# Fewer certain experts, tests ahead of the last one, and an accumulation moved from GpSimd to VectorE

## The chip, the cores and the metric

The kernel runs on one core of a Trainium2 chip. The metric is the device time of one execution in microseconds (us), the median of several runs. The engines are TensorE (PE in the profile, with PEld for its weight loads), VectorE (DVE), ScalarE (ACT), GpSimd (POOL) and SyncE (SP). SP issues nearly all large transfers from device memory.

## What is computed

The reference is a network of two layers on 256 tokens of 1024 numbers in float32. In both layers a mixer is followed by a layer of 16 experts.

```python
for i in range(DEPTH):                                   # 2 layers
    sh1, sc1, g1, sh2, sc2, g2 = split(silu(c) @ mod_w[i] + mod_b[i])     # the modulation, 6 vectors
    h = x * (1 + sc1) + sh1
    y = attention_group_mixer(h, ...) if i == 0 else hyena_mixer(h, ...)
    x = layer_norm(ALPHA * x + g1 * y)
    f = moe_ffn(x * (1 + sc2) + sh2, router_w, router_bias, w_gate[i], w_up[i], w_down[i])
    x = layer_norm(ALPHA * x + g2 * f)
# moe_ffn: each token goes to the 2 best experts of its best group of 4; for an expert e
#   out += weight * ((silu(xb @ w_gate[e]) * (xb @ w_up[e])) @ w_down[e])
# hyena_mixer: h @ w_in, a short convolution, two long convolutions through the spectra of a small filter network, @ w_out
```

One expert has three matrices of 4 MB. How many tokens each expert gets follows from the inputs. The reference's routing, worked out on its own inputs, gives experts 0 and 1 of layer 0 28 and 1 tokens, and the other fourteen, sorted, 171, 128, 42, 41, 30, 29, 16, 13, 6, 3, 2, 1, 1, 0. In layer 1 it is 2 and 1, and 215, 184, 33, 30, 18, 14, 6, 5, 3, 1, 0, 0, 0, 0.

## The kernel before

**Stages.** The first 230 us are attention with the modulation woven in. `mod_vec` fetches each of ten modulation vectors in four 1 MB tiles; step `i` scales the two halves of a tile (`k`) by a column of `cz` and adds them up. Four of the eight products per vector are multiplied and added on VectorE (L268, the pairs in `MOD_DVE`), four are scaled on ScalarE (L270), and two of those are then added on GpSimd (L272). GpSimd also adds the two partial sums (L274). The attention units (`diff_scores`, `win_scores`) stand between these steps in the same queues. Then come `mixer_tail` (projection, norm, routing), the experts of layer 0 (`moe`), the hyena mixer, its `mixer_tail`, the experts of layer 1 and the last norm.

**Experts.** `moe` takes positions `p`. Positions 0 and 1 are experts 0 and 1. The two most loaded others are done densely in pieces, beside p = 1 to 8 (`PIECES`: `dense_up` on odd p, four more tiles; `dense_down` on even p, two more tiles). Positions 2 to 13 are the other twelve, by falling load, so p = 9, 10, 11, 12, 13 stand for 3, 2, 1, 1, 0 tokens in layer 0 and 1, 0, 0, 0, 0 in layer 1. An expert takes twelve tiles of 1 MB, eight for gate and up, four for down. Positions 0 to 11 (`RARE = 12`) always run. They are pipelined: `E.up()`, the `back()` of the one before, the `pick()` and `turn_in()` of the next one, dense piece, `E.weights_in()`, `E.down()`. Positions 12 and 13 stand in `rare`, each inside a test on its number of tokens (`tc.If`, L793), the second nested in the first. Every engine takes the test in its own queue.

**Tiles.** Weight tiles go through a ring of 12 slots, with `MORE` extra slots during `moe` (3 in layer 0, 5 in layer 1). SP issues loads in program order through `load` (L143) and waits at each until its slot is free, so it runs ahead by as many tiles as there are slots.

**Fillers.** In layer 0, `filler(p)` computes the spectra of the hyena filter. `filt_mlp` runs at p = 0, and eight pieces `filt_spec` (L1186, L1195, the copies L163 and a store to `spec`) run at the positions in `FILL`. They take PSUM banks from the rotating counter `abank()`, six per piece. `spec_loads` brings each piece's inputs through GpSimd's queue, one piece ahead.

**After the experts.** The first tile of the hyena weights (`hy_w_in`) is asked for at the end of `moe` (`NAHEAD = 1`), the others in `win_loads`. At the start of the hyena stage the residual `xs` is multiplied and shifted by a norm's gain (L1339, L1340).

Of the kernel before, what the change touches and what calls it, by code (L numbers as in the profile page):

```python
# [12 lines left out]
ALU = mybir.AluOpType  # L13
AX = mybir.AxisListType
ET = mybir.EngineType
# [13 lines left out]
MORE = [3, 5]  # L29
# [11 lines left out]
FILL = [0, 8, 9, 9, 10, 10, 11, 11]  # L41
# [5 lines left out]
MOD_DVE = {(1, 0), (2, 0), (2, 1), (3, 0)}  # L47

RARE = 12
NAHEAD = 1  # L50
# [26 lines left out]
def emit(tc, I, O):  # L77
# [4 lines left out]
    with es:  # L82
# [170 lines left out]
        def mod_vec(l, v):  # L253
# [7 lines left out]
            def step(i):  # L261
                w = st[i]
                c_ = [cz[:, 2 * i + k, 0:1] for k in range(2)]
                if i == 0:
                    st["acc"] = w
                for k in range(2):
                    if (i, k) in MOD_DVE:
                        dve.scalar_tensor_tensor(out=st["acc"][:, 0], in0=w[:, k], scalar=c_[k], in1=st["acc"][:, 0], op0=ALU.mult, op1=ALU.add)  # L268
                    else:
                        act.activation(w[:, k], w[:, k], AF.Copy, scale=c_[k])  # L270
                        if i:
                            pool.tensor_tensor(out=st["acc"][:, 1], in0=st["acc"][:, 1], in1=w[:, k], op=ALU.add)  # L272
                if i == 3:
                    pool.tensor_tensor(out=st["acc"][:, 1], in0=st["acc"][:, 1], in1=st["acc"][:, 0], op=ALU.add)  # L274
# [449 lines left out]
        def moe(l, h2, R, first, filler):  # L724
            with tc.tile_pool(name=f"mp{l}", bufs=2, reuse_waits="tile") as mp:
# [26 lines left out]
                hid, last = {}, None  # L752
                for p in range(RARE):
                    if p == 0:
                        E.w = first
                    else:
                        ix = number(1, place(p), [ET.SP], NE - 1) if p > 1 else 1
                        E.w = expert_loads(l, ix, have=second if p == 1 else (), most=8)
                        if p in PIECES:
                            r, half, down = PIECES[p]  # L760
                            dw = dense_loads(l, number(1, 2 + r, [ET.SP], NE - 1), half, down)
                        E.w = expert_loads(l, ix, have=E.w)
                    E.up()
                    if last:
                        last.back()
                    nxt = expert(p + 1) if p + 1 < RARE else None
                    if nxt:
                        nxt.pick()
                    if p == 0:
                        for t in range(2):  # L770
                            dve.tensor_tensor(out=xs[:, t, :], in0=h2[:, t, :], in1=lng, op=ALU.mult)
                            for hf in range(2):
                                s_ = slice(512 * hf, 512 * hf + 512)
                                dve.tensor_tensor(out=xs[:, t, s_], in0=xs[:, t, s_], in1=lnb[hf], op=ALU.add)
                    E.turn_mid()
                    if p in PIECES:
                        if down:
                            dense_down(mp, E.bank, dw, hid[r], R["wtP"][:, :, 2 + r:3 + r], g2b)
                        else:
                            hid[r] = dense_up(mp, E.bank, dw, h2T)  # L780
                    if filler:
                        filler(p)
                    if nxt:
                        nxt.turn_in()
                    E.weights_in()
                    E.down()
                    E, last = nxt, E
                last.back()

# [21 lines left out]
                def beyond():  # L811
# [3 lines left out]
                    with tc.For_i(0, NE):  # L815
# [12 lines left out]
                        dve.tensor_copy(ints[:, :, 0:15], ni[:, :, 1:16])  # L828
                        for i, nm in enumerate(("rankP", "wtP")):
                            dve.tensor_copy(mv_[:, 2 * i:2 * i + 2], R[nm])  # L830
                            dve.tensor_copy(R[nm][:, :, 0:15], mv_[:, 2 * i:2 * i + 2, 1:16])
                        dve.tensor_copy(mv_[:, 4], cap)
                        dve.tensor_copy(cap[:, 0:15], mv_[:, 4, 1:16])
                rare(RARE)
# [343 lines left out]
        def filt_spec(o, q):  # L1178
# [4 lines left out]
            for t in range(2):  # L1183
                b = abank()
# [16 lines left out]
        def filler(p):  # L1201
# [3 lines left out]
            for i in [i for i, p_ in enumerate(FILL) if p_ == p]:  # L1205
                filt_spec(*oq[i])
# [6 lines left out]
        with tc.tile_pool(name="fp", bufs=1, reuse_waits="tile", side="right") as fp:  # L1213
            wi = I["hy_w_in"][0]
            moe(0, h2, R, first, filler)
            ws0 = [win_tile(0, i, -1) for i in range(NAHEAD)]
# [3 lines left out]
        if True:  # L1220
            hTh = hm([128, KC, N], "hTh")
            with tc.tile_pool(name="s1a", bufs=1) as sa:
# [65 lines left out]

                def fwd(src, sp_, s):
# [20 lines left out]
                    for c, op in enumerate((ALU.add, ALU.subtract)):  # L1310
                        dve.tensor_tensor(out=Y[:, c], in0=prods[0], in1=prods[1], op=op)
# [26 lines left out]
                for t in range(2):  # L1338
                    dve.tensor_tensor(out=xs[:, t, :], in0=xs[:, t, :], in1=gb[:, 0], op=ALU.mult)  # L1339
                    dve.tensor_tensor(out=xs[:, t, :], in0=xs[:, t, :], in1=gb[:, 1], op=ALU.add)  # L1340
# [104 lines left out]
```

## Time and profile before

| | us |
|---|---|
| median of 3 runs (1373.05 to 1373.99) | 1373.26 |
| the profiled execution | 1371.12 |
| its span, first to last instruction | 1369.4 |
| PE busy in the span | 1201.0 |
| VectorE busy | 568.1 |
| ScalarE busy | 233.1 |
| GpSimd busy | 122.8 |

All durations below come from the one profiled execution, which is 2.1 us below the median. A busy PE is not a PE at its peak, and a high share over the whole span says little here, since the stages have different limits. So the profile is read by stage.

### The profile page before, as it was taken

The page shows a single profiled execution, that of the slowest core. Times are in us where ns is not written, and L with a number is a line of the kernel's source. Part 1 is how long each engine was busy: PE and PEld are TensorE (multiplying, and loading weights), DVE is VectorE, ACT ScalarE, POOL GpSimd, SP SyncE. Part 2 cuts the span into 40 slices and gives each one's busy share as a digit, 9 for nine tenths or more (in the row PEclk, how much of TensorE's full clock was granted, in tenths as well). Part 3 has the DMA queues.
Part 4 walks back from the last instruction along what each step waited for, and adds up shares of the span by engine and source line. Part 5 has one row for each costly group of instructions (what it writes and reads, how often), then busy time and mean ns, then how long its engine had stood idle before and what let it go on. Part 6 is the DMA issues. An engine that isn't in the chain of part 4 may idle for free. (4 is left out here: it accounts for less than half of the span.)

```text
span 1369.4 us, 21175 instructions
## 1 busy us (share of the span) xinstructions
PE 1201.0 (88%) x8630; PEld 716.2 (52%) x8630; DVE 568.1 (41%) x1127; ACT 233.1 (17%) x441; POOL 122.8 (9%) x118
## 2 busy tenths in 40 slices
PE   5999887958999999899786699996999999999864
PEld 1444444425746566484554387853744747465421
DVE  2466988373031222303333479937122131321313
ACT  2344556130000000000000263203000000000000
POOL 1244433110000000000111000001000000000000
PEclk9999999978999999999999799997999999999985
DMA  9999775576998999999999764687999899999994
GB/s 327 398 369 340 289 285 198 203 275 267 383 402 334 362 401 408 401 391 402 399 400 407 281 229 177 264 311 274 404 409 402 335 403 378 402 403 407 409 408 174
DMA packets 139803, 469.37 MB, mean 343 GB/s; under 512 B 8655, under 2 KB 10279, under 8 KB 139696
## 3 DMA queue, kind: packets, MB, share of 16 engines
q1 hardware_dynamic: 133696, 451.93, 85.0%
q0 software_dynamic: 4928, 13.44, 2.9%
q10 hardware_dynamic: 1072, 2.54, 0.5%
q8 instruction: 71, 1.16, 0.3%
q14 instruction: 36, 0.29, 0.1%
HBM read 462.62 MB, written 5.26 MB: 342 GB/s over the span
## 5 line engine op out<-in xcount | busy, mean ns | idle before, releaser
L642 PE MATMUL acc<-w,xe 128*32 128x256 f32 (+1 forms) x2944 | 228.5, 414 | 12.6 <-DMA w<-in_exp_w_up 5.1
L705 PE MATMUL acc<-xnT,w 128*128 128x256 f32 x1024 | 222.5, 379 | 1.1 <-DVE xs L686 1.1
L705 PEld LDWEIGHTS acc<-xnT,w 128*128 128x128 f32 x1024 | 193.9, 190 | 27.5 <-DVE xs L686 1.3
L642 PEld LDWEIGHTS acc<-w,xe 128*32 128x32 f32 (+1 forms) x2944 | 104.5, 116 | 121.9 <-issue 54.7
L661 PE MATMUL acc<-w,aT 128*32 128x256 f32 (+1 forms) x1472 | 122.8, 421 | 18.2 <-DVE stg L163 8.4
L717 PE MATMUL acc<-w,hid 128*128 128x512 f32 x256 | 111.4, 593 | 0.3 <-DVE xs L686 0.3
L661 PEld LDWEIGHTS acc<-w,aT 128*32 128x32 f32 (+1 forms) x1472 | 52.8, 116 | 75.8 <-issue 26.1
L708 DVE TENSOR_TENSOR hid<-hid,acc 128x256 f32<-128x256 f32 x32 | 13.4, 420 | 189.6 <-ACT hid L707 189.6
L686 DVE TENSOR_TENSOR xs<-xs,acc 128x512 f32<-128x512 f32 x100 | 62.6, 682 | 53.7 <-PE acc L680 53.4
L717 PEld LDWEIGHTS acc<-w,hid 128*128 128x128 f32 x256 | 48.0, 190 | 58.3 <-issue 56.9
L268 DVE SCALAR_TENSOR_TENSOR w<-w,cz 128x1024 f32<-128x1024 f32 x40 | 69.4, 1734 | 13.1 <-DMA w<-in_mod_w 11.4
L646 DVE TENSOR_TENSOR ac<-ac,acc 128x256 f32<-128x256 f32 (+1 forms) x25 | 11.6, 464 | 151.4 <-PE acc L642 151.4
L918 PE MATMUL acc<-w,hT 128*128 128x512 f32 (+1 forms) x192 | 72.6, 524 | 1.7 <-DVE mr L163 1.7
L1268 PE MATMUL acc<-hTh,w 128*128 128x256 f32 x320 | 59.4, 285 | 0.1
L272 POOL TENSOR_TENSOR w<-w 128x1024 f32<-128x1024 f32 x20 | 49.5, 2477 | 104.4 <-ACT w L270 71.3
L645 ACT ACTIVATE ac<-acc 128x256 f32<-128x256 f32 (+1 forms) x25 | 10.4, 418 | 282.4 <-PE acc L642 282.4
L161 ACT ACTIVATE xg<-mis 128x256 f32<-128x256 f32 (+1 forms) x25 | 10.4, 417 | 270.3 <-PE mis L610 270.2
L719 DVE SCALAR_TENSOR_TENSOR do<-acc,wtP,g2b 128x512 f32<-128x512 f32 x32 | 24.0, 751 | 67.7 <-PE acc L717 67.7
L918 PEld LDWEIGHTS acc<-w,hT 128*128 128x128 f32 x192 | 34.9, 190 | 32.2 <-issue 27.7
L610 PE MATMUL mis<-h,Pu 128*32 128x256 f32 (+1 forms) x368 | 38.5, 434 | 14.7 <-DVE PT L163 9.7
L1268 PEld LDWEIGHTS acc<-hTh,w 128*128 128x128 f32 x320 | 49.4, 188 | 2.3 <-ACT ed L1296 1.3
L680 PE MATMUL acc<-yb,PT 32*128 32x256 f32 (+1 forms) x368 | 45.6, 443 | 4.4 <-DVE yb L666 4.4
(351 smaller groups left out, 1398.0 us busy)
## 6 DMA issues: line engine op xcount, KB each, us to landing
w<-in_exp_w_up SPq DMA_DIRECT2D x116, 1024.0 KB, 18.1
w<-in_exp_w_gate SPq DMA_DIRECT2D x116, 1024.0 KB, 18.1
w<-in_exp_w_down SPq DMA_DIRECT2D x116, 1024.0 KB, 13.8
w<-in_mod_w SPq DMA_DIRECT2D x40, 1024.0 KB, 8.2
w<-in_hy_w_in SPq DMA_DIRECT2D x12, 1024.0 KB, 9.7
w<-in_attn_w_in SPq DMA_DIRECT2D x9, 1024.0 KB, 10.5
w<-in_mod_w SPq DMA_DIRECT2D x16, 512.0 KB, 10.8
w<-in_attn_w_out SPq DMA_DIRECT2D x4, 1024.0 KB, 5.0
```

The lines of the kernel that those rows point to most:

```text
L268: dve.scalar_tensor_tensor(out=st["acc"][:, 0], in0=w[:, k], scalar=c_[k], in1=st["acc"][:, 0], op0=ALU.mult, op1=ALU.add)
L272: pool.tensor_tensor(out=st["acc"][:, 1], in0=st["acc"][:, 1], in1=w[:, k], op=ALU.add)
L610: pe.matmul(gb[S * j:S * j + S, 0:nn], Pu[:, t, 0:S], self.h2[:, t, nn * j:nn * j + nn], start=(t == 0), stop=(t == 1), tile_position=(0, ...
L642: pe.matmul(A[m][S * j:S * j + S, 0:nn], self.xe[:, kc, :], w[:, nn * j:nn * j + nn], tile_position=(0, S * j), start=(kc == 0), stop=(kc ...
L661: pe.matmul(y[S * q:S * q + S, 0:nn], lhs, w[:, nn * q:nn * q + nn], tile_position=(0, S * q), start=(kc == 0), stop=(kc == KC - 1))
L680: pe.matmul(o, self.PT[r, 128 * t:128 * t + 128], self.yb[r, 0:nn], start=True, stop=True, tile_position=(S * q, 0))
L686: dve.tensor_tensor(out=x_, in0=x_, in1=o, op=ALU.add)
L705: pe.matmul(b[:, N * m:N * m + N], ws[m][kc // 4][:, kc % 4, 128 * fb:128 * fb + 128], h2T[:, kc, :], start=(kc == 0), stop=(kc == KC - 1))
L717: pe.matmul(b, hid[:, fb, 128 * t:128 * t + 128], ws[fb // 2][:, fb % 2, s_], start=(fb == 0), stop=(fb == 3))
L719: dve.scalar_tensor_tensor(out=o, in0=b, scalar=wt[:, t], in1=g2b[:, s_], op0=ALU.mult, op1=ALU.mult)
L918: pe.matmul(bank[:, 0:width], hT[:, kc, 128 * t:128 * t + 128], st["w"][kc // per][:, kc % per, :], start=(kc == 0), stop=(kc == KC - 1))
L1268: pe.matmul(b[:, 0:N], w_, m, start=(kc == 0 and i == 0), stop=(kc == KC - 1 and i == len(ps) - 1))
```

## The change

`RARE` becomes 10, so positions 10 to 13 are nested tests, and they stand ahead of position 9 (`NEST`), the last certain one. The `back()` of position 8 comes ahead of them, and position 9 is picked after them. `NAHEAD` becomes 4: four hyena tiles are asked for behind position 9's. `MORE` for layer 0 is 4. `FILL` spreads the pieces over p = 0, 0, 4, 6, 8, 8, 9, 9, and these take banks 3, 4 and 5 of the expert. In `mod_vec` ScalarE scales only the two halves of the first tile, and VectorE does all else. The `xs` operations of the hyena stage are placed behind the last operation of the first `fwd`. `beyond` now rotates its tables fully, since it is no longer the last in its layer.

```diff
-MORE = [3, 5]
+MORE = [4, 5]
-FILL = [0, 8, 9, 9, 10, 10, 11, 11]
+FILL = [0, 0, 4, 6, 8, 8, 9, 9]
-MOD_DVE = {(1, 0), (2, 0), (2, 1), (3, 0)}
-RARE = 12
-NAHEAD = 1
+RARE = 10
+NEST = 9
+NAHEAD = 4
...
-                    if (i, k) in MOD_DVE:
-                        dve.scalar_tensor_tensor(out=st["acc"][:, 0], in0=w[:, k], scalar=c_[k], in1=st["acc"][:, 0], op0=ALU.mult, op1=ALU.add)
+                    if i:
+                        dve.scalar_tensor_tensor(out=st["acc"][:, k], in0=w[:, k], scalar=c_[k], in1=st["acc"][:, k], op0=ALU.mult, op1=ALU.add)
                     else:
                         act.activation(w[:, k], w[:, k], AF.Copy, scale=c_[k])
-                        if i:
-                            pool.tensor_tensor(out=st["acc"][:, 1], in0=st["acc"][:, 1], in1=w[:, k], op=ALU.add)
                 if i == 3:
-                    pool.tensor_tensor(out=st["acc"][:, 1], in0=st["acc"][:, 1], in1=st["acc"][:, 0], op=ALU.add)
+                    dve.tensor_tensor(out=st["acc"][:, 1], in0=st["acc"][:, 1], in1=st["acc"][:, 0], op=ALU.add)
...
                 for p in range(RARE):
+                    if p == NEST:
+                        last.back()
+                        last = None
+                        rare(RARE)
+                        E = expert(p)
+                        E.pick()
+                        E.turn_in()
...
-                    nxt = expert(p + 1) if p + 1 < RARE else None
+                    nxt = expert(p + 1) if p + 1 < RARE and p + 1 != NEST else None
...
-                        filler(p)
+                        filler(p, E.bank)
...
-                rare(RARE)
...
-                b = abank()
+                b = bank[4 + t]
...
-                b = abank()
+                b = bank[3 + c % 3]
...
-                    ws = [win_tile(s, i) if s or i >= NAHEAD else ws0[i] for i in range(2)]
+                    ws = [ws0[j] if j < NAHEAD else win_tile(s, j % 2) for j in (2 * s, 2 * s + 1)]
...
-                for t in range(2):
-                    dve.tensor_tensor(out=xs[:, t, :], in0=xs[:, t, :], in1=gb[:, 0], op=ALU.mult)
-                    dve.tensor_tensor(out=xs[:, t, :], in0=xs[:, t, :], in1=gb[:, 1], op=ALU.add)
+                with tc.issue_after(st_["last"]):
+                    for t in range(2):
+                        dve.tensor_tensor(out=xs[:, t, :], in0=xs[:, t, :], in1=gb[:, 0], op=ALU.mult)
+                        dve.tensor_tensor(out=xs[:, t, :], in0=xs[:, t, :], in1=gb[:, 1], op=ALU.add)
```

## Rows read from the trace of the kernel before

**Rows 1.** Busy time by stretch: start:end, length, busy us (count) per engine, granted clock, DMA.

```profile
117.00:232.00 115.00, 94.00 (x445) 52.45 (x443) 106.28 (x179) 68.59 (x135) 48.31 (x24) 1.00 0.73 266
...
411.00:445.00 34.00, 34.00 (x158) 22.72 (x155) 4.01 (x7) 1.96 (x4) 0.00 (x0) 1.00 0.84 334
...
650.00:768.00 118.00, 91.43 (x980) 56.76 (x976) 37.83 (x80) 5.12 (x11) 15.80 (x26) 0.96 1.01 394
...
813.00:892.00 79.00, 74.34 (x489) 60.99 (x488) 78.38 (x112) 28.44 (x47) 0.00 (x0) 0.99 0.59 218
...
1257.00:1351.00 94.00, 70.63 (x776) 31.45 (x776) 19.69 (x37) 5.12 (x11) 0.00 (x0) 0.89 0.98 391
```

**Rows 2.** DMA issues of the page: out<-in, engine, count, KB each, us to landing.

```profile
w<-in_exp_w_up SPq DMA_DIRECT2D x116, 1024.0 KB, 18.1
```

**Rows 3.** Instructions in time, VectorE, 136 to 146 us: start, us, what, idle before.

```profile
136.48 2.30 DVE L987 TENSOR_SCALAR mx<-mx 128x2 f32<-128x2 f32 x1
...
140.57 0.14 DVE L987 TENSOR_SCALAR mx<-mx 128x2 f32<-128x2 f32 x1
...
141.95 1.27 DVE L268 SCALAR_TENSOR_TENSOR w<-w,cz 128x1024 f32<-128x1024 f32 x1
...
145.09 3.44 DVE L268 SCALAR_TENSOR_TENSOR w<-w,cz 128x1024 f32<-128x1024 f32 x1
```

**Rows 4.** The same view for GpSimd, same stretch.

```profile
145.08 2.37 POOL L272 TENSOR_TENSOR w<-w 128x1024 f32<-128x1024 f32 x1 [6.32 <-issue]
```

**Rows 5.** VectorE's groups, 117 to 240 us: count, busy us, mean ns, idle before.

```profile
L268 DVE SCALAR_TENSOR_TENSOR w<-w,cz 128x1024 f32<-128x1024 f32 x24 | 38.5, 1603 | 0.1
...
L393 DVE TENSOR_SCALAR fold<-modc 128x8 f32<-128x8 f32 x2 | 1.8, 914 | 0.0
```

**Rows 6.** GpSimd's busy time of L272 alone, then of L274 alone, 117 to 232 us.

```profile
117.00:232.00 115.00, 29.91 (x12) 1.00 0.73 266
...
117.00:232.00 115.00, 14.14 (x6) 1.00 0.73 266
```

**Rows 7.** PE in time at p = 11 of layer 0: fillers, then down.

```profile
724.38 1.89 PE L1186 MATMUL acc<-fwo,hs 128*128 128x256 f32 x8
...
740.76 3.66 PE L661 MATMUL acc<-w,aT 128*32 128x256 f32 x64 [2.68 <-DVE stg L163]
```

**Rows 8.** SP's issues in time around position 12 of layer 0.

```profile
715.57 1.20 SPq L143 DMA_DIRECT2D w<-in_exp_w_gate  x1
...
737.37 14.56 SPq L143 DMA_DIRECT2D w<-in_exp_w_down  x4
773.84 2.48 SPq L143 DMA_DIRECT2D w<-in_hy_w_in  x4
```

**Rows 9.** The tests, 700 to 780 us: durations min/median/max ns, first and last start; SP's waits.

```profile
L793 SPq COMPARE_BRANCH  x3: 38/48/50, 714.6 to 768.8; - x3
...
SPq L143 <- PEq L793: 4.7, 1, 4.7
```

**Rows 10.** PE and VectorE in time, end of layer 0's experts.

```profile
768.27 1.07 PE L661 MATMUL acc<-w,aT 128*32 128x256 f32 x16 [1.55 <-SPq L793]
769.89 1.15 PE L680 MATMUL acc<-yb,PT 32*128 32x256 f32 x16 [0.55 <-DVE yb L666]
...
771.05 2.48 DVE L686 TENSOR_TENSOR xs<-xs,acc 128x512 f32<-128x512 f32 x4 [1.22 <-PE acc L680]
...
778.92 0.41 DVE L386 TENSOR_SCALAR hT<-mis,fold 128x128 f32<-128x128 f32 x1 [0.36 <-DMA w<-in_hy_w_in]
```

**Rows 11.** PE in time, layer 1: end of p = 8, then p = 10, then p = 11.

```profile
1279.22 0.71 PE L680 MATMUL acc<-yb,PT 32*128 32x256 f32 x6 [0.55 <-DVE yb L666]
...
1305.95 1.07 PE L642 MATMUL acc<-w,xe 128*32 128x256 f32 x16 [1.01 <-DMA w<-in_exp_w_gate]
...
1350.57 1.93 PE L661 MATMUL acc<-w,aT 128*32 128x256 f32 x16 [0.58 <-SPq L793]
```

**Rows 12.** VectorE in time, start of the hyena stage.

```profile
781.77 1.23 DVE L1339 TENSOR_TENSOR xs<-xs,gb 128x1024 f32<-128x1024 f32 x1 [1.28 <-DMA gb<-in_ln_g]
```

More of the change, by code (lines that the diff above doesn't have):

```diff
@@ L831, in beyond @@
                             dve.tensor_copy(R[nm][:, :, 0:15], mv_[:, 2 * i:2 * i + 2, 1:16])
+                            dve.tensor_copy(R[nm][:, :, 15:16], mv_[:, 2 * i:2 * i + 2, 0:1])
                         dve.tensor_copy(mv_[:, 4], cap)
                         dve.tensor_copy(cap[:, 0:15], mv_[:, 4, 1:16])
-                rare(RARE)
+                hid, last = {}, None
+                for p in range(RARE):
+                    if p == NEST:
[5 more added lines that the diff above has]
+                        E.turn_in()
+                    if p == 0:
+                        E.w = first
+                    else:
+                        ix = number(1, place(p), [ET.SP], NE - 1) if p > 1 else 1
+                        E.w = expert_loads(l, ix, have=second if p == 1 else (), most=8)
+                        if p in PIECES:
+                            r, half, down = PIECES[p]
+                            dw = dense_loads(l, number(1, 2 + r, [ET.SP], NE - 1), half, down)
+                        E.w = expert_loads(l, ix, have=E.w)
+                    E.up()
+                    if last:
+                        last.back()
+                    nxt = expert(p + 1) if p + 1 < RARE and p + 1 != NEST else None
+                    if nxt:
+                        nxt.pick()
+                    if p == 0:
+                        for t in range(2):
+                            dve.tensor_tensor(out=xs[:, t, :], in0=h2[:, t, :], in1=lng, op=ALU.mult)
+                            for hf in range(2):
+                                s_ = slice(512 * hf, 512 * hf + 512)
+                                dve.tensor_tensor(out=xs[:, t, s_], in0=xs[:, t, s_], in1=lnb[hf], op=ALU.add)
+                    E.turn_mid()
+                    if p in PIECES:
+                        if down:
+                            dense_down(mp, E.bank, dw, hid[r], R["wtP"][:, :, 2 + r:3 + r], g2b)
+                        else:
+                            hid[r] = dense_up(mp, E.bank, dw, h2T)
+                    if filler:
+                        filler(p, E.bank)
+                    if nxt:
+                        nxt.turn_in()
+                    E.weights_in()
+                    E.down()
+                    E, last = nxt, E
@@ L835, in moe @@
+                last.back()
                 act.activation(dumm, epsc[:, 0:1], AF.Sqrt)
@@ L1199, in emit, with filler @@
         oq = [(o, q) for q in range(D // FQ) for o in range(2)]
-        def filler(p):
+        def filler(p, bank):
             if p == 0:
```

47 lines of the change are left out of this document (8 added, 39 removed).

## The prediction

> **What bounds the kernel now.** I read the busy time by stretch first, because every stretch has another limit. In the second half of the attention stage VectorE is busy for 106.28 of 115 us while the DMA runs at 0.73 [rows 1], so VectorE's queue sets that time. (The rows stand in order of time.) In the dense pieces at the start of layer 0's experts PE is busy without a gap (34.00 of 34.00) and the DMA falls to 0.84 [rows 1]. From 650 us to the end of layer 0's experts the DMA is full (1.01 at 394 GB/s) and PE has 27 us of idle time in 118 [rows 1]. The end of layer 1 looks the same (0.98, with 23 us of PE idle in 94) [rows 1]. In the hyena stage VectorE is busy for 78.38 of 79 us, beside 74.34 of PE [rows 1].
>
> The list of DMA issues then tells how many experts ran. `w_up` has 116 issues of 1 MB [rows 2], four per expert, so 29 experts in two layers. That fits the routing: position 12 ran in layer 0 (one token) and not in layer 1, which leaves 15 and 14. So in layer 1 the positions 10 and 11, with no token, are loaded and multiplied for nothing.
>
> The views in order of time, of SP, PE and VectorE around the tests, come last: they show what a test does to the stream of loads.
>
> **Part 1: two experts fewer in layer 1.** A tile comes every 2.62 us: the seventh tile of p = 10 at 1305.95 and the twelfth of p = 11 at 1350.57 are 17 tiles apart [rows 11]. Two experts are 24 tiles, 63 us. But the test is now in the middle of the stream. In layer 0 the last tile of position 12 lands at 768.27, and SP, which issued it long before, issues nothing more until 773.84, when it waited for PE's side of the test [rows 8 to 10]. PE's last matmul ends at 769.89 + 1.15 = 771.04, so the next load goes out 2.8 us after PE is through, and that tile is there at 778.92, 5.1 us after its issue [rows 10]. I take this for a rule of the kernel: a load behind a test's end waits for PE to have done everything ahead of it, since the slot's last readers stand inside the test. Queued behind SP's waiting load are all twelve tiles of position 9. All engines' work for it waits for these.
>
> In layer 1 the `back()` of p = 8 starts at 1279.22 and takes 1.15 us when not interleaved [rows 10, 11], so PE is done at 1280.4. SP issues at 1283.2, and the twelfth tile lands 5.1 + 11 x 2.62 = 33.9 us later, at 1317.1. Before, the last tile lands at 1350.57 [rows 11]. What follows it is the same, so layer 1 gives back **33.5 us**: 63 us of loads less 29 us in which the DMA stands idle, as PE finishes a dense piece for which the tiles came long before. If loads were not held, it would be 63 less some 5 us for a new start, 58.
>
> Beside this, a rule on the price of the branch. The trace has 2.8 us from PE's last matmul to SP's issue. The Trainium skill (Advanced Engine Details and Errata, Control Flow Timing) gives a compare-and-branch about 108 ns; by it the two joins would cost about 5 us less in all, an estimate. The sum goes by the trace.
>
> **Part 2: the experts of layer 0.** The bytes stay the same here; the order changes. Entering a test holds nothing up: SP branched at 714.6 and issued the first tile of p = 12 at 715.57, while PE was still at p = 11 (its `down` came at 740.76) [rows 7 to 9]. So positions 10, 11 and 12 stream as before, though unpipelined; PE's idle 27 us of 118 [rows 1] cover that. The last tile of p = 12 now comes twelve tiles earlier, 31.5 us. It also comes some 4 us earlier because about three fewer filler pieces store their 0.5 MB in this full stretch (1.3 us each at 394 GB/s) [rows 1]. That is 768.3 - 31.5 - 4 = 732.8. SP is released 5.6 us later, as before (768.27 to 773.84), at 738.4. Position 9 needs 33.9 us and some 2.6 for two pieces' stores: 774.9. From the last tile to the end of the residual is 768.27 to 773.53, 5.3 us [rows 10]. The experts end at 780.2 instead of 773.5: **+7 us**.
>
> Two fillers now stand in position 9, the last one. Before, two pieces took 740.76 - 724.38 = 16.4 us between up and down [rows 7], 2.7 of it for a PSUM bank. If they stay behind the up, the tail grows by 13.7 + 2.7 less the 10.5 us of four down tiles, some +6 us. Their new banks (3 to 5) free them from the up (banks 0, 1) and the down (bank 2), so I expect them between the up tiles, of which PE uses 1.07 us in each 2.6 [rows 11]: 0. Range 0 to +8.
>
> The fillers at p = 4 and 6 go into the stretch where PE has no idle time [rows 1]. A piece is at most 8.2 us there (half of 16.4), at least nothing if the DMA, ahead by a whole ring, stays the limit: together 0 to +16. The second filler at p = 0 hides in the waits of `filt_mlp`, whose chain of small steps leaves PE idle, and p = 0's down no longer needs its banks: 0 to +6. One more slot of lookahead is worth up to one tile, -2.6. Together I take **+2**, near the low end, since the DMA, not PE, ends the layer.
>
> **Part 3: modulation.** In the 115 us that VectorE sets, GpSimd runs 12 + 6 additions [rows 6]. They become 12 multiply-adds of 1.27 us [rows 3] and 6 additions of 1.23 (same shape [rows 12]), 22.6 us more on VectorE. What goes away is a stall. An L268 that starts together with a GpSimd addition takes 3.44 us and not 1.27, and the addition itself is 2.37 [rows 3, 4]. A two-element L987 takes 2.30 instead of 0.14 [rows 3]. Eleven groups of VectorE have means above their unblocked time (from L268, 24 x (1.603 - 1.27) = 8.0 us, to L393, 2 x 0.76 = 1.5) [rows 5], 26.7 us in all. So VectorE has 4 us less to do, and no queue waits for GpSimd: **-5 us**. Range: -12 if the softmax chain also tightens, +10 if only the 8 us of L268 and a few more stalls go.
>
> A rule that speaks against this: the Trainium skill (Perfetto Trace Analysis, Optimizing Scalar/DVE Operations) says that work may be moved off a saturated VectorE, even to GpSimd; this change does the reverse. The same place adds that the two share a port, and SBUF — State Buffer (SBUF: two separate sides) calls it an exclusive lock that blocks the loser for the whole instruction. The trace agrees with the lock, 3.44 against 1.27 us. By the first rule alone the sum would be 27 us worse.
>
> **Part 4: the hyena stage.** The first `xs` operation at 781.77 held VectorE back by 1.28 + 1.23 us while PE waited for the transposed input [rows 12]. Without it the stage starts 2.5 us earlier. But four of these operations, 4.9 us, move to where VectorE is full [rows 1], so it may end 2.4 us later. The four tiles asked for early were hidden by the norm for all but a moment. I take **0**, range -2.5 to +5.
>
> **The sum.** Against the profiled execution: 1371.1 - 5 + 7 + 2 + 0 - 33.5 = 1341.6. The median stands 2.1 us above it: **1343**.
>
> **The rivals.** *Loads run on behind the test.* If the slots of position 9 were free of PE's side of the test, layer 1 would give 58 instead of 33.5, and layer 0 about 8 less: 1311. For it speaks only that the trace shows one kind of load behind a test; the 4.7 us that SP waited for PE [rows 9] speaks against. Chance 0.13.
>
> *The first rule on VectorE.* If VectorE gains the 22.6 us and the stalls were not on its path, the total is 1343 + 27 = 1370, within 0.2% of before. Against it stands the 106.28 of 115 us. Chance 0.03.
>
> *Slower: every nested test holds SP like a join.* Then positions 10, 11, 12 and 9 of layer 0 would each start with an empty queue. The first would wait for p = 8 and its two fillers, as in layer 1 some 29 us and 14 more, the second and third for 5.3 + 2.8 + 2.5 = 10.6 us each. That is +64 us in layer 0, 1407. It is slower from the point where the holds exceed the 30 us that the rest gains, so already with the first. Against it: the load at 715.57, 1 us after SP's branch [rows 8, 9]. Chance 0.05.
>
> *The change does not skip.* If rank 10 of layer 1 held a token, nothing would be saved and the join lost, some +10 us. The routing says none. Chance 0.01.
>
> **How the numbers follow.** My forecast has the remaining 0.78. Its own bounds add to about 1325 and 1365; within it 1361 leaves out little. The low end goes to 1316, towards the first rival. About 0.2% is what a measurement of this kernel can tell from no change. Faster by more: 0.78 + 0.13 = 0.91; within: 0.03; slower: 0.06.
>
> **What would show it.** Layer 1 must have 12 experts (27 in all, `w_up` x108), and layer 0 15. In layer 1 SP should issue nothing for some 20 us ahead of position 9, its first tile going out about 3 us behind PE's `back()`; an issue right after the branch makes the first rival right. In layer 0 the same hole should stand ahead of position 9, and none ahead of 10, 11 and 12. L268 should have one duration near 1.27, and 60 of them. The fillers of p = 9 should stand between the up matmuls. The forecast is wrong if the hole is missing, or if PE in the dense pieces pushes the whole stream of layer 0 back by the fillers' full time.

## The result and the profile after

| us | before | after |
|---|---|---|
| median of the runs | 1373.45 (1373.05 to 1373.99) | 1324.30 (1321.83 to 1327.74) |
| the profiled execution | 1371.12 | 1325.61 |
| its span | 1369.4 | 1323.8 |

The ratio of the medians is 0.9644, with an interval of 0.962 to 0.9668. The kernel is 3.6% faster. The forecast said 1343 in a range of 1316 to 1361: right in sign and inside the range, but 19 us too high. Measured at the same milestones of the two traces, the span splits as follows, each figure good to some 0.1 us.

| stretch | before | after | change | forecast |
|---|---|---|---|---|
| attention, to the first projection matmul | 234.5 | 216.6 | -17.9 | -5 |
| from there to the end of `dense_down` at p = 8, layer 0 | 407.5 | 409.0 | +1.5 | +2 |
| from there to the end of layer 0's last residual operation | 131.5 | 144.1 | +12.6 | +7 |
| from there to the projection of layer 1 | 123.0 | 122.4 | -0.6 | 0 |
| from there to the end of `dense_down` at p = 8, layer 1 | 378.6 | 370.8 | -7.8 | 0 |
| from there to PE's last `back()` | 80.0 | 47.1 | -32.9 | -33.5 |
| tail | 14.3 | 13.8 | -0.5 | 0 |
| sum | 1369.4 | 1323.8 | -45.6 | -29.5 |

**The experts.** The page's list of DMA issues, after (out<-in, engine, count, KB each, us to landing), shows 27 experts, 108 / 4, in place of 29 [rows 2]:

```profile
w<-in_exp_w_up SPq DMA_DIRECT2D x108, 1024.0 KB, 16.9
```

**Attention.** Of the kernel after, the instructions of line 267, with minimum, median and maximum in ns:

```profile
L267 DVE SCALAR_TENSOR_TENSOR w<-w,cz x60: 1251/1276/2020, 52.9 to 221.8; 128x1024 f32<-128x1024 f32 x60
```

There are 60, and the median is the unblocked 1.27 us; before, the mean was 1.603 [rows 5]. The slowest, 2.02 us at 181.63, starts just behind another operation of GpSimd (L1100, 1.04 us at 181.53). Busy time by stretch, from the first `diff_scores` matmul to the projection, before and then after (columns as in rows 1):

```profile
116.70:234.50 117.80, 96.77 (x469) 54.20 (x468) 107.49 (x181) 69.24 (x137) 48.31 (x24) 1.00 0.73 267
```

```profile
115.30:216.60 101.30, 94.14 (x466) 54.80 (x465) 93.74 (x189) 56.38 (x125) 3.98 (x6) 1.00 0.77 290
```

VectorE runs eight instructions more and is busy for 13.8 us less. It no longer sets the time alone: PE has 94.14 and VectorE 93.74 of 101.3 us.

**Layer 1.** SP's waits of the kernel after, 1230 to 1300 us (who waited for what: us in all, times, longest), then its issues in time:

```profile
SPq L738 <- DVEq L752: 19.5, 1, 19.5
```

```profile
1271.77 0.39 SPq L142 DMA_DIRECT2D w<-in_exp_w_gate  x1
...
1280.58 9.44 SPq L142 DMA_DIRECT2D w<-in_exp_w_down  x4
```

PE in time, of the same stretch:

```profile
1249.04 13.90 PE L714 MATMUL acc<-w,hid 128*128 128x512 f32 x32
...
1267.08 1.15 PE L677 MATMUL acc<-yb,PT 32*128 32x256 f32 x16 [0.55 <-DVE yb L663]
...
1278.47 1.93 PE L639 MATMUL acc<-w,xe 128*32 128x256 f32 x16 [3.17 <-DMA w<-in_exp_w_gate]
...
1306.45 1.86 PE L658 MATMUL acc<-w,aT 128*32 128x256 f32 x16 [0.57 <-DMA w<-in_exp_w_down]
```

The hole stands where the forecast put it. `back()` ends at 1268.23, the first tile goes out 3.5 us later, and the whole of position 9 then waits tile by tile. But the row of SP's wait names another cause. SP does not stand at a load (line 142) that waits for PE. It stands at line 738, which reads the number of the next expert into a register, and it waits there for VectorE's mark of the test (line 752). `beyond` rotates the tables inside the test, VectorE writes them, and a read of the table behind the test must wait for that, taken or not. VectorE gives its mark when the four residual additions of position 8's `back()` are through, at 1270.72 (VectorE in time):

```profile
1268.24 2.48 DVE L683 TENSOR_TENSOR xs<-xs,acc 128x512 f32<-128x512 f32 x4 [1.22 <-PE acc L677]
```

**Layer 0.** PE in time around the nested tests, after:

```profile
669.58 1.15 PE L677 MATMUL acc<-yb,PT 32*128 32x256 f32 x16 [0.55 <-DVE yb L663]
673.52 1.94 PE L607 MATMUL mis<-h,Pu 128*32 128x256 f32 x16 [2.80 <-DVE Pu L601]
...
693.61 1.15 PE L677 MATMUL acc<-yb,PT 32*128 32x256 f32 x16 [0.55 <-DVE yb L663]
...
713.37 3.66 PE L658 MATMUL acc<-w,aT 128*32 128x256 f32 x64 [0.53 <-ACT aT L160]
717.58 1.15 PE L677 MATMUL acc<-yb,PT 32*128 32x256 f32 x16 [0.55 <-DVE yb L663]
...
759.61 1.93 PE L658 MATMUL acc<-w,aT 128*32 128x256 f32 x16 [3.35 <-DMA w<-in_exp_w_down]
762.66 1.93 PE L658 MATMUL acc<-w,aT 128*32 128x256 f32 x16 [1.11 <-DMA w<-in_exp_w_down]
```

Each nested expert takes 24.0 us of PE from `back()` to `back()`, since nothing of it overlaps with the next. The third `down` (713.37) waits for ScalarE and not for a tile: position 12's last tile landed at 711.5, and the DMA then has nothing to move (busy time by stretch, columns as in rows 1):

```profile
712.00:714.00 2.00, 1.07 (x14) 0.62 (x18) 0.34 (x1) 0.38 (x1) 0.00 (x0) 1.00 0.00 0
```

The third expert ends at 718.73, and SP's first issue for position 9 follows 3.4 us later (SP's issues in time, after):

```profile
722.15 0.39 SPq L142 DMA_DIRECT2D w<-in_exp_w_gate  x1
...
742.81 18.86 SPq L142 DMA_DIRECT2D w<-in_hy_w_in  x4
```

### The profile page after: what moved, and what is told of

The parts are those of the page before. It is cut to its first block, busy times and chain, and to the rows that moved or that the text cites. A ratio compares the mean times of both kernels' runs of the same rounds, so it can differ in the third digit from the quotient of the medians.

```text
span 1323.8 us, 20044 instructions
## 1 busy us (share of the span) xinstructions
PE 1184.8 (89%) x8170; PEld 707.2 (53%) x8170; DVE 550.0 (42%) x1131; ACT 209.3 (16%) x415; POOL 48.3 (4%) x88
## 5 line engine op out<-in xcount | busy, mean ns | idle before, releaser
L639 PE MATMUL acc<-w,xe 128*32 128x256 f32 (+1 forms) x2688 | 220.2, 434 | 13.1 <-DMA w<-in_exp_w_gate 5.2
L702 PEld LDWEIGHTS acc<-xnT,w 128*128 128x128 f32 x1024 | 193.9, 190 | 26.7 <-DVE xs L683 0.6
L639 PEld LDWEIGHTS acc<-w,xe 128*32 128x32 f32 (+1 forms) x2688 | 100.9, 121 | 122.5 <-issue 65.6
L658 PE MATMUL acc<-w,aT 128*32 128x256 f32 (+1 forms) x1344 | 116.1, 419 | 11.5 <-DMA w<-in_exp_w_down 7.9
L658 PEld LDWEIGHTS acc<-w,aT 128*32 128x32 f32 (+1 forms) x1344 | 48.3, 115 | 64.6 <-issue 26.2
L267 DVE SCALAR_TENSOR_TENSOR w<-w,cz 128x1024 f32<-128x1024 f32 x60 | 75.7, 1287 | 10.9 <-DMA w<-in_mod_w 10.9
L643 DVE TENSOR_TENSOR ac<-ac,acc 128x256 f32<-128x256 f32 (+1 forms) x23 | 10.7, 467 | 154.2 <-PE acc L639 154.2
L683 DVE TENSOR_TENSOR xs<-xs,acc 128x512 f32<-128x512 f32 x92 | 57.4, 681 | 40.2 <-PE acc L677 40.1
L607 PE MATMUL mis<-h,Pu 128*32 128x256 f32 (+1 forms) x336 | 36.5, 487 | 17.4 <-DVE Pu L601 13.3
L704 ACT ACTIVATE hid<-acc 128x256 f32<-128x256 f32 x32 | 12.3, 384 | 208.7 <-PE acc L702 208.7
L1273 PE MATMUL acc<-hTl,w 128*128 128x256 f32 x160 | 44.8, 280 | 0.0
## 6 DMA issues: line engine op xcount, KB each, us to landing
w<-in_exp_w_down SPq DMA_DIRECT2D x108, 1024.0 KB, 13.2
```

The lines of the kernel that those rows point to most:

```text
L267: dve.scalar_tensor_tensor(out=st["acc"][:, k], in0=w[:, k], scalar=c_[k], in1=st["acc"][:, k], op0=ALU.mult, op1=ALU.add)
L607: pe.matmul(gb[S * j:S * j + S, 0:nn], Pu[:, t, 0:S], self.h2[:, t, nn * j:nn * j + nn], start=(t == 0), stop=(t == 1), tile_position=(0, ...
L639: pe.matmul(A[m][S * j:S * j + S, 0:nn], self.xe[:, kc, :], w[:, nn * j:nn * j + nn], tile_position=(0, S * j), start=(kc == 0), stop=(kc ...
L658: pe.matmul(y[S * q:S * q + S, 0:nn], lhs, w[:, nn * q:nn * q + nn], tile_position=(0, S * q), start=(kc == 0), stop=(kc == KC - 1))
L683: dve.tensor_tensor(out=x_, in0=x_, in1=o, op=ALU.add)
L702: pe.matmul(b[:, N * m:N * m + N], ws[m][kc // 4][:, kc % 4, 128 * fb:128 * fb + 128], h2T[:, kc, :], start=(kc == 0), stop=(kc == KC - 1))
```

## The experiments

The theory was the forecast's: loads of position 9 wait behind the tests, and VectorE gains by losing GpSimd's stalls. The first two runs split the change in two.

**The modulation alone.** The kernel before, with only this edit:

```diff
-                    if (i, k) in MOD_DVE:
-                        dve.scalar_tensor_tensor(out=st["acc"][:, 0], ...in1=st["acc"][:, 0], ...)
+                    if i:
+                        dve.scalar_tensor_tensor(out=st["acc"][:, k], ...in1=st["acc"][:, k], ...)
...
-                            pool.tensor_tensor(out=st["acc"][:, 1], in0=st["acc"][:, 1], in1=w[:, k], op=ALU.add)
...
-                    pool.tensor_tensor(out=st["acc"][:, 1], ...)
+                    dve.tensor_tensor(out=st["acc"][:, 1], ...)
```

> The kernel before with the modulation edit alone: all sums on VectorE, no additions on GpSimd. Theory: the stalls of VectorE behind GpSimd's additions set the second half of the attention stage. In the changed kernel the projection behind it starts at 216.6 us instead of 234.5, 17.9 us earlier, and this edit makes all of that. Nothing later takes it back, so the total is 1373 - 18 = 1355 (1351 to 1359). Rival one: the edit gives the 5 us of the prediction and the rest came from elsewhere: 1368. Rival two: the experts of layer 0 are limited by their loads, so an earlier start is lost there: 1371 to 1373, with the projection still at 217.

Measured: 1351.89 us (1349.79 to 1353.48), ratio 0.9846 (0.9808 to 0.9885). The projection starts at 216.5, as in the kernel after. The edit is worth some 20 us by itself.

**All but the modulation.** The kernel after, with the modulation of before (the same diff, reversed).

> The changed kernel with the modulation as it was before (sums shared between VectorE, ScalarE and GpSimd), all else changed. Theory: the two parts add up, so the total is 1324 + 18 = 1342 (1338 to 1347), with the projection at 234 to 235 us again and L268 at 3.4 us wherever a GpSimd addition overlaps it. Rival: the parts overlap, since later stages are limited by loads that start at fixed times: 1324 to 1330.

Measured: 1342.77 us (1342.73 to 1343.96), ratio 0.9783 (0.9747 to 0.982), and the projection starts at 235.7. The product of the two ratios is 0.9632, beside 0.9644 of the whole change: the parts add up. The pair also bounds what the edits of the hyena stage give together, the place of the `xs` operations and the tiles asked for early. From layer 0's last residual operation to the projection of layer 1 it is 122.7 us without them (the run above) and 122.4 with them (here); they were not tried apart.

**No additions on GpSimd.** The kernel before without line 272's and line 274's additions. The modulation vectors then keep one of their eight products, the routing changes, and only the attention stage can be read.

```diff
-                            pool.tensor_tensor(out=st["acc"][:, 1], in0=st["acc"][:, 1], in1=w[:, k], op=ALU.add)
+                            pass
...
-                    pool.tensor_tensor(out=st["acc"][:, 1], in0=st["acc"][:, 1], in1=st["acc"][:, 0], op=ALU.add)
+                    pass
```

> The kernel before with GpSimd's 30 additions of the modulation left out, nothing in their place, so the modulation and all that follows from it (the routing too) is not computed; only the attention stage is read, not the total. Theory: VectorE stalls for each addition that overlaps it, 31 us between 117 and 234 us, and sets that stage. Without the additions L268 takes 1.26 to 1.32 us each time, and the projection starts at 205 to 213 us (234.5 before, 216.6 with the additions on VectorE). Rival: the gain came from shorter chains between engines and not from stalls; then the stage ends at 225 to 235, as VectorE's own work is unchanged.

The projection starts at 212.8, and the stage takes 98.9 us. Line 268 and the stretch (views and columns as above):

```profile
L268 DVE SCALAR_TENSOR_TENSOR w<-w,cz x24: 1269/1276/1286, 115.8 to 207.5; 128x1024 f32<-128x1024 f32 x24
```

```profile
113.90:212.80 98.90, 95.56 (x470) 55.48 (x469) 80.59 (x181) 68.92 (x137) 3.97 (x6) 0.98 0.84 315
```

With the same 181 instructions as before, VectorE is busy for 80.59 us and not 107.49. So the stalls were 26.9 us. No L268 is longer than 1.29 us. PE is now busy for 95.56 of 98.9 us, so little is left that VectorE could still give.

**A memset in place of each addition.** This asks whether any work on GpSimd stalls VectorE, or only work that reads. The same parts of the sums are left out.

```diff
-                            pool.tensor_tensor(out=st["acc"][:, 1], in0=st["acc"][:, 1], in1=w[:, k], op=ALU.add)
+                            pool.memset(w[:, k], 0.0)
...
-                    pool.tensor_tensor(out=st["acc"][:, 1], in0=st["acc"][:, 1], in1=st["acc"][:, 0], op=ALU.add)
+                    pool.memset(st["acc"][:, 0], 0.0)
```

> As the run without GpSimd's additions, but a memset of the same size (128 x 1024) stands on GpSimd where each addition stood, with the same waits; the sums are again not computed, and only the attention stage is read. Theory: what blocks VectorE is that GpSimd's instruction reads the same memory through a path that both use, so a memset, which reads nothing, leaves VectorE alone: L268 at 1.26 to 1.35 us, and the projection at 205 to 215 us. Rival: any GpSimd instruction of that length blocks VectorE: L268 up to 3.4 us again and the projection at 225 to 236.

The projection starts at 217.7, and the stage takes 100.4 us. Line 268, then VectorE and GpSimd in time:

```profile
L268 DVE SCALAR_TENSOR_TENSOR w<-w,cz x24: 1272/1277/1286, 119.2 to 211.8; 128x1024 f32<-128x1024 f32 x24
```

```profile
140.92 1.00 DVE L987 TENSOR_SCALAR mx<-mx 128x2 f32<-128x2 f32 x1
140.99 1.28 DVE L268 SCALAR_TENSOR_TENSOR w<-w,cz 128x1024 f32<-128x1024 f32 x1
```

```profile
140.91 1.00 POOL L272 MEMSET w<- 128x1024 f32 x1 [6.70 <-ACT w L270]
```

The theory is right on L268 and not on the projection: 217.7 lies above the expected 205 to 215, though far below the rival's 225, as 3.4 of the 4.9 us to the run above arose ahead of the stage (it begins at 117.3 and not at 113.9). No L268 was delayed by a memset, though several started beside one. The small L987 was: it began with the memset and ended with it, 1.00 us in place of 0.16. Two more L987 and one L1019 took 0.33 to 0.73 us beside a memset. So there are two kinds of stall. The Trainium skill (SBUF — State Buffer, SBUF: two separate sides) says that a VectorE instruction with two SBUF inputs contends only with a GpSimd instruction that reads SBUF, and the same page (Who interferes with whom) counts the single-source kinds among those that may take both ports. The trace agrees with both: L268 reads two tiles and was blocked by additions alone (3.44 us [rows 3]), L987 reads one and was blocked by both. A memset is also short, 0.95 us where the addition takes 2.37 [rows 4], so this run alone doesn't tell how much is due to its length; that L268 was untouched doesn't hang on it.

**Tests last.** The kernel after with the nested tests behind position 9, so that no load of an expert stands behind a test.

```diff
-                    if p == NEST:
-                        last.back()
-                        last = None
-                        rare(RARE)
-                        E = expert(p)
-                        E.pick()
-                        E.turn_in()
...
-                    nxt = expert(p + 1) if p + 1 < RARE and p + 1 != NEST else None
+                    nxt = expert(p + 1) if p + 1 < RARE else None
...
+                rare(RARE)
```

> The changed kernel with the nested tests behind position 9, as the last thing in each layer; 10 to 13 are still tested. Theory: the test ahead of position 9 costs a hole in the stream of loads, since no load behind the test goes out until PE has done all work ahead of it. In layer 1 the tiles of p = 8 were there at 1251.1 us and the first tile of p = 9 at 1278.3; without the hole position 9 ends 20 to 25 us earlier. In layer 0 position 9 runs in the stream, the tested ones end at some 751 us and the hyena mixer starts 12 to 15 us earlier although its tiles are asked for behind the tests. Total 1324 - 22 - 14 = 1288 (1280 to 1296). Rival: the hole is PE's lag behind the loads and stays wherever the test stands, and the hyena tiles come late: 1315 to 1330.

Measured: 1291.25 us (1289.79 to 1295.2), ratio 0.9402 (0.9367 to 0.9437). This beats both kernels. PE in time at the end of layer 1:

```profile
1259.16 3.66 PE L658 MATMUL acc<-w,aT 128*32 128x256 f32 x64
...
1273.89 3.66 PE L658 MATMUL acc<-w,aT 128*32 128x256 f32 x64 [0.53 <-ACT aT L160]
1278.10 1.15 PE L677 MATMUL acc<-yb,PT 32*128 32x256 f32 x16 [0.55 <-DVE yb L663]
```

From `dense_down` to the end of `back()` it is 20 us, in place of 47.1; no tile of position 9 is waited for. By stretches, against the kernel after: attention +2.2, layer 0 -15.5, from there to the projection of layer 1 +5.1 (the hyena tiles now stand behind the tests, and PE waits 2.5 us for the second of them; the rest of the 5.1 was not traced), layer 1 and the tail -22.2. The sum is -30.4, the difference of the two spans. So the place of the tests in the stream costs some 30 us, and the change wins in spite of it.

**Position 9's first tiles in slots that no test reads.** By the forecast's reason for the hold, this must let four tiles of layer 0 and five of layer 1 go out early.

```diff
-                        E.w = expert_loads(l, number(1, place(p), [ET.SP], NE - 1))
+                        E.w = expert_loads(l, number(1, place(p), [ET.SP], NE - 1), slot=-1)
...
+                        if p == NEST:
+                            all_slots(MORE[l])
-                        E.w = expert_loads(l, ix, have=second if p == 1 else (), most=8)
+                        E.w = expert_loads(l, ix, have=second if p == 1 else (), most=MORE[l] if p == NEST else 8, new=p == NEST)
```

> The changed kernel with other slots for the weights: the tested positions use only the 12 ring slots, and the first tiles of position 9 (4 in layer 0, 5 in layer 1) get the extra slots, whose last readers all stand ahead of the tests. Theory: a load behind a test waits because the last readers of its slot stand inside the test, so it needs PE's mark at the test's end. Then these 4 and 5 tiles go out as soon as SP itself is past the test, about 20 us earlier in layer 1, and position 9 ends 5 x 2.6 = 13 us earlier there. In layer 0 up to 10 us are gained the same way, and up to 8 lost as the tested experts have 12 slots for 16: 1324 - 13 - 2 = 1309 (1302 to 1316). Rival: SP itself is held at the test's end, whatever slot the load has: no issue before PE's back(), 1322 to 1334.

Measured: 1331.11 us (1329.29 to 1332.62), ratio 0.9699 (0.9663 to 0.9736): a miss, and slower than the change itself. SP's waits, 1230 to 1300 us:

```profile
SPq L738 <- DVEq L752: 19.4, 1, 19.4
```

The wait is as long as before this edit, so slots were not what held SP, or not they alone. The 4.3 us that layer 0 loses (557.4 us from the projection to its end, beside 553.1) may be the price of the four extra slots that the nested experts no longer had; that was not tried apart.

**The number read ahead of the tests.** If the register read is the only hold, all twelve tiles go out early. If slots hold as well, nothing changes.

```diff
+                        ahead = number(1, place(p), [ET.SP], NE - 1)
                         rare(RARE)
...
-                        ix = number(1, place(p), [ET.SP], NE - 1) if p > 1 else 1
+                        ix = ahead if p == NEST else number(1, place(p), [ET.SP], NE - 1) if p > 1 else 1
```

> The changed kernel, but SP reads the number of position 9's expert ahead of the tests. In the trace of the changed kernel, SP's read of that number behind the test (L738) waits 19.5 us for VectorE's mark at the test's end, since code inside the innermost test writes the table that it reads. Theory: that read holds SP, and behind it stands a second hold, the slots, whose last readers on PE stand inside the tests. Then taking away the first wait alone moves the first issue by less than 1 us (PE's back() ends at 1268.2, plus some 3 us): 1324 (1319 to 1328). Rival: the read was the only hold. Then the tiles go out about 20 us earlier in layer 1 and some 8 us earlier in layer 0: 1296 (1290 to 1304).

Measured: 1322.75 us (1319.57 to 1323.97), ratio 0.9648 (0.9612 to 0.9685): no gain. SP's waits in the same stretch:

```profile
SPq L142 <- PEq L752: 19.3, 1, 19.3
```

Now SP stands at the load, and it waits for PE's mark of the test: the forecast's hold, hidden until then behind the other.

**Both.** The two edits together.

> Both at once: the number is read ahead of the tests, and the first 4 and 5 tiles of position 9 have slots that no tested position reads (as in the run with own slots, which took 1331). Theory of two holds: with both gone the first 5 tiles of layer 1 go out at some 1252 us instead of 1277, and the other seven follow from 1277 on, so position 9 ends 5 x 2.6 = 13 us earlier; layer 0 gains up to 4 x 2.6 = 10 us: 1331 - 13 - 7 = 1311 (1305 to 1319). If the read was the only hold, 1300 to 1306, with all tiles going out at once. If neither, 1328 to 1334.

Measured: 1311.46 us (1310.92 to 1314.37), ratio 0.958 (0.9545 to 0.9616). SP's waits and issues in time:

```profile
SPq L142 <- PEq L752: 16.2, 1, 16.2
```

```profile
1251.49 0.38 SPq L142 DMA_DIRECT2D w<-in_exp_w_gate  x1
...
1254.03 0.37 SPq L142 DMA_DIRECT2D w<-in_exp_w_gate  x1
1270.78 0.37 SPq L142 DMA_DIRECT2D w<-in_exp_w_up  x1
```

Five tiles go out 17 to 19 us ahead of the sixth, which has no slot of its own and waits for PE. In layer 1 the stretch from `dense_down` to `back()` takes 32.8 us for 47.1 after, which is about five tiles at 2.6. Layer 0 gains nothing: 553.3 us from the projection to its end, beside 553.1. Its four tiles go out at 722.2, but the nested experts, with 12 slots, end 6.5 us later (508.6 us from the projection to their last `back()`, for 502.2), and SP's fifth tile goes out at 730.58 only. So there are two holds, and either of them suffices.

**The fillers of positions 4 and 6 later.** This tests the term of +2 us. `FILL` is the list of positions.

```diff
-FILL = [0, 0, 4, 6, 8, 8, 9, 9]
+FILL = [0, 0, 8, 8, 8, 9, 9, 9]
```

> The changed kernel with the pieces of p = 4 and 6 moved to 8 and 9: FILL is 0, 0, 8, 8, 8, 9, 9, 9. Theory: a piece takes 5.5 us of PE in the dense stretch, where PE has no idle time, so the dense_down of p = 8 ends some 9 to 11 us earlier (625.6 in the changed kernel). But the third piece at p = 8 delays the tested positions, which PE limits too (24 us each), by some 8 us, and the third at p = 9 waits for its inputs and stretches the tail by up to 5: 1324 (1319 to 1329), no net gain. Rival: loads and not PE limit the dense stretch, so its pieces were free there and the move only adds: p = 8 ends at 623 to 626 still, total 1332 to 1340.

Measured: 1323.06 us (1321.08 to 1326.95), ratio 0.9651 (0.9618 to 0.9685), the same as with the change. PE in time at p = 8 of layer 0, first after and then this run:

```profile
611.75 13.90 PE L714 MATMUL acc<-w,hid 128*128 128x512 f32 x32
```

```profile
603.71 13.90 PE L714 MATMUL acc<-w,hid 128*128 128x512 f32 x32
```

From the projection (216.6 and 218.8) to the end of this piece it is 409.0 us after and 398.8 here. So two fillers among the dense pieces do cost 10.2 us of PE's time there. But the layer's end, 553.1 and 552.0 us from the projection, moved by 1.1 only: what the two save ahead of the tests they take again behind them.

**The same list, tests last.** If the 10 us were given back by the hold alone, they should appear where no hold is.

> The tests behind position 9 (1291 in the earlier run) with the same late pieces (0, 0, 8, 8, 8, 9, 9, 9). Theory: PE limits layer 0 from p = 1 to the last tested position, so moving PE's work within that stretch changes nothing: 1291 (1287 to 1295). Rival: at p = 8 and 9 PE waits for loads, so pieces there are free and 9 to 11 us are gained: 1281.

Measured: 1300.13 us (1298.51 to 1300.36), ratio 0.9489 (0.9459 to 0.952): a miss for both expectations, and slower than with the early fillers (0.9402). Busy time and DMA from 630 to 660 us, tests last, then this run:

```profile
630.00:660.00 30.00, 26.92 (x251) 16.34 (x250) 12.05 (x24) 0.38 (x1) 5.40 (x9) 1.00 1.03 399
```

```profile
630.00:660.00 30.00, 26.58 (x251) 16.64 (x252) 9.91 (x21) 0.77 (x2) 5.80 (x10) 0.94 0.84 314
```

Layer 0 ends 544.7 us after its projection, 7.1 later than with the early list (537.6). With three fillers each at p = 8 and 9, position 9's `down` ends at 470.7 us after the projection and not at 460.1, SP waits longer for its slots (from 600 to 770 us 44.4 us behind `down` matmuls, with the early list 29.5), and the DMA falls to 314 GB/s. Behind that come the nested experts at 24 us each, with no slack in which to recover it.

## Why the prediction came out as it did

**The sum, -29.5, and its range.** The measured -45.6 differs by three misses: attention 12.9 us too small, 7.8 us unforeseen in layer 1, and layer 0 5.6 us worse. That the range held is partly luck. The bounds of the terms, simply added, give 1329 (-7 modulation, -4.6 fillers and lookahead, -2.5 hyena) to 1391 (+15, +8, +20, +5), not 1325 to 1365. The measured 1324.3 lies below both low ends; it is inside only because the low end was taken down to 1316 towards the first rival, which the runs refute. Layer 1's -33.5 and layer 0's +7 had no bounds of their own.

**Layer 1, -33.5: right, for a reason only half right.** The size of the hole, its place and its end behind PE's `back()` came out: -32.9 at that place. "A load behind a test's end waits for PE to have done everything ahead of it" holds, as the run with the number read ahead shows. But ahead of it stands the read at line 738, which waits for VectorE. The forecast took the wait for one of slots alone. Its number survived because the two marks are less than 1 us apart: from the end of `back()` to the first issue it is 2.8 us where PE's mark alone holds (1268.39 to 1271.20 in the run with the number read ahead), and 3.5 with both. That is luck: the 2.5 us of VectorE's residual additions, for which the read waits, stand nowhere in the forecast. It would have failed for any edit that relied on the slots, as the expectation for that run did. The row to look at was in the diff and not in the trace: `beyond` "now rotates its tables fully".

**Unforeseen: -7.8 in the dense pieces of layer 1.** PE in time, before and then after:

```profile
1207.22 0.83 PE L610 MATMUL mis<-h,Pu 128*32 128x256 f32 x9 [1.49 <-DVE PT L163]
...
1215.97 27.79 PE L705 MATMUL acc<-xnT,w 128*128 128x256 f32 x128
...
1255.96 1.07 PE L610 MATMUL mis<-h,Pu 128*32 128x256 f32 x16 [0.71 <-DVE PT L163]
...
1261.18 13.90 PE L717 MATMUL acc<-w,hid 128*128 128x512 f32 x32
```

```profile
1174.05 1.07 PE L607 MATMUL mis<-h,Pu 128*32 128x256 f32 x16 [0.70 <-DVE PT L162]
...
1207.14 27.79 PE L702 MATMUL acc<-xnT,w 128*128 128x256 f32 x128
...
1249.04 13.90 PE L714 MATMUL acc<-w,hid 128*128 128x512 f32 x32
```

Before, the picks of later positions (L610 and what follows) were done ahead, between the matmuls of p = 7 and 8, where PE has no free time. From the piece at p = 7 to that at p = 8 it was 45.2 us and is now 41.9. Position 9 is now picked behind the tests, and 10 and 11 not at all; the pick at 1174.05 is that of p = 8. The run with only the modulation, which keeps both picks, has 378.7 us in this stretch; the tests last, which keep one, 375.3; the change 370.8. In layer 0 the tests last, with one pick more than the change, have 411.9 us in this stretch for 409.0. If the saving of both picks is as large there as in layer 1, it pays for most of the fillers at p = 4 and 6, so that the stretch came out at +1.5 with the forecast at +2. That term was right by two errors: the fillers cost 10.2 and not 2, as the run without them there shows.

**Attention, -5: the sign right, a third of the size.** The stalls were well counted, 26.7 us against 26.9. The failed term is the work that replaces them. The 22.6 us for 12 multiply-adds and 6 additions took over GpSimd's count in the old stretch. In the new, shorter one stand 33 multiply-adds for 24 and 5 additions for none. That is 14 more (and six small instructions fewer), and VectorE's busy time rises from 80.59 us without any to 93.74, by 13.2. The other four come after the projection has begun. VectorE so gained 13.8 us, and the stage 16.5, as VectorE's idle time fell from 10.3 to 7.6 us. The rival by which VectorE would gain 22.6 us of path falls: the modulation alone is faster by 1.5%.

**Layer 0, +7: too low by 5.6, and the part that fits fits by luck.** SP's release was to be 738.4 against 642.1, 96.3 us behind the piece of p = 8, and is 722.15 against 625.6, 96.5. But the way there was another. The forecast let the loads set it, with PE's idle 27 us covering the experts that are no longer pipelined. The last tile then was to land at 732.8, 90.7 us behind the piece, and SP to go on 5.6 us later. It landed at 711.5, after 85.8 us, and SP waited 10.7 us more, since PE set the end: 20 us of fillers and `down` to 645.5, then three times 24.0 us. Two errors of 5 us cancel. What follows was to take 41.8 us and took 47.6. The DMA, from 722 to 765 us (queue, kind: packets, MB, share; then issues with KB each and us to landing):

```profile
q0 software_dynamic: 672, 2.23, 13.6%
...
gbf<-in_ln_g POOLq DMA_DIRECT2D x1, 512.0 KB, 9.6
gbf<-in_ln_b POOLq DMA_DIRECT2D x1, 512.0 KB, 11.6
```

The forecast allowed for two pieces' stores (1 MB). GpSimd's queue moves 2.23 MB in this time, since the norm's `gbf` (1 MB) falls into it too. At 383 GB/s the 1.2 MB more are 3.1 us, of the 4.0 that the time from SP's first issue (722.15) to the last tile on PE (762.66) is longer than forecast (40.5 for 36.5). This reading was argued and not tried. The rest, 1.8 us, is the tail behind the last tile.

**The fillers of position 9, 0: right.** They stand between the `up` matmuls, 722 to 747 us, and `down` waits for tiles, not for them.

**Hyena, 0: right.** The stage begins 7.2 us after layer 0's end and not 10.2, and ends within 0.6, so most of the earlier start is lost again, as the forecast said.

**The rivals.** Loads that run on behind the test: no, by the two waits. Every nested test holding SP: no; the loads of the nested experts streamed (DMA at 1.03 from 669.6 to 693.6 us), and the two holds stand ahead of position 9 alone.

*The price of the branch.* It is short on SP and long on PE. These are the rows of line 752 in layer 1 (durations min/median/max in ns), first two of the kernel after, then one of the run with the number read ahead:

```profile
L752 SPq COMPARE_BRANCH  x1: 58/58/58, 1237.0 to 1237.0; - x1
L752 PEldq COMPARE_BRANCH  x1: 3600/3600/3600, 1267.6 to 1267.6; - x1
```

```profile
L752 PEldq COMPARE_BRANCH  x1: 3340/3340/3340, 1267.7 to 1267.7; - x1
```

The Trainium skill (Advanced Engine Details and Errata, Control Flow Timing) gives a compare-and-branch about 108 ns. SP's 58 ns is below that; PE's row at the skipped test is thirty times as long, so the rule by which the two joins would cost 5 us less fails here. Where PE's mark alone holds, this row ends at 1271.06, 2.7 us behind the last matmul, and SP issues at 1271.20: it is nearly all of the 2.8 us that the forecast took from the trace without a cause. (Before, PE's row took 3.33 us and ended at 773.70, just ahead of SP's issue at 773.84.) With both holds, 2.5 of the 3.5 us are VectorE's additions and 1.0 the read of the number and the issue.

## What to carry to other kernels

A run-time test in a stream of loads costs what stands behind it, so put it last, or give what follows its own slots and read its registers ahead; removing one of two holds shows nothing. Before an addition is moved between VectorE and GpSimd, look for instructions that are far above their own minimum: here GpSimd's additions in one stage held VectorE for 26.9 us, and the operations that took their place there cost it 13.2. Count what runs ahead of its place, too: the picks of skipped work stood in a stretch that PE set.

## What the runs showed of the hardware

A VectorE multiply-add of two SBUF tiles waits for a whole GpSimd addition (3.44 us for 1.27) and not for a memset, while a two-element L987 waits for both (2.30 us and 1.00 us for 0.14 to 0.16). The wait goes both ways: a GpSimd addition (L272) that started 0.03 us behind an L268, at 135.32, took 3.44 us and not 2.36. In all, GpSimd's additions held VectorE for 26.9 of the 107.49 us that it was busy in that stage.

On PE the compare-and-branch of a test that was entered took 65 to 86 ns, and that of a skipped one 3.3 to 3.7 us before and after, in both layers. In layer 0 of the run with both edits, with the DMA full beside it, it took 6.8 us (723.67 to 730.45), which is why the fifth tile there came so late. What PE does in this time no run shows.

In the nested experts, where PE has 6 us of gaps in each 24, the granted clock fell; busy time from 650 to 770 us, after:

```profile
650.00:770.00 120.00, 88.14 (x968) 46.89 (x960) 27.29 (x64) 5.89 (x13) 6.32 (x11) 0.77 0.90 350
```

Before, the same part had 0.96 [rows 1]. The 16 matmuls of a pick (L607) took 1.94 us in a nested expert (673.52) and 1.07 between dense pieces (1174.05), near the ratio of the two levels of 1.2 and 2.4 GHz.
